# The root of a norm, by a logarithm and an exponential on ScalarE instead of a square root on ScalarE and a reciprocal on VectorE

## The chip, the core and the metric

The kernel runs on one core of a Trainium2 chip. Its metric is the device time of one execution in microseconds (us), the median of several. Five engines work side by side, each with its own queue that it takes strictly in order: TensorE (PE, and PEld for its weight loads), VectorE (DVE), ScalarE (ACT), GpSimd (POOL) and SyncE (SP), the last two mostly issuing transfers. ScalarE looks a function up in a table; a row named ACT_TABLE_LOAD is the instruction that puts another table in place.

## What is computed

Two layers of a hybrid attention and expert network over 512 latent tokens and 256 context tokens of width 1024. What the change touches is the norm, used for rows, for the low-rank projections and for every head:

```python
def rms_norm(x, g):
    x32 = x.astype(jnp.float32)
    y = x32 * lax.rsqrt(jnp.mean(x32 * x32, axis=-1, keepdims=True) + EPS)
    return (y * g.astype(jnp.float32)).astype(x.dtype)
```

Each layer: norm and modulation of the tokens, one input projection, latent attention (queries and keys normed per head) and windowed attention (likewise), softmaxes, an output projection, a second norm with modulation, and then expert retrieval: a product-key search picks 16 of 16384 experts for each of 8 heads, whose rows of `u` and `v` are gathered, dotted with the token and added up. For some token tiles all experts are computed densely instead.

## The kernel before

Tokens go in tiles of 128 (two of context, four latent). A layer has two parts.

The **first part** runs generators for each tile: `KV` and `Q` (norm, projection, low-rank step, head norms, transposes into `kT`, `qT`, `skT`, `sqT`), `A` (attention: scores, `soft`, transposes, values), `O` (output projection, second norm), `R` (product-key search, L606 to L653) and `G` (the choice of experts). Which instruction stands where in each engine's queue is decided by a scheduler when the program is built; the code's order is only its starting point. In the same part the gathered expert rows (L752 to L776) run whenever a tile has made its choice: POOL issues one indirect gather per row (L754), DVE makes the dot with the token (L758, `gv`) or the weighted sum (L768, `vacc`). Layer 0 starts with no such rows to do, since no tile has chosen; layer 1 begins with 40 rows left over from layer 0 and then has none until its first tile has chosen.

The **second part** of a layer streams all experts (L858 on) for the dense tiles, with the remaining gathered rows in between, in an order written out by hand. There are no norms in it.

All 88 norms end in one helper, `rstd_of` (L239): a square root on ACT with the mean and the epsilon folded into scale and bias (L241), then a reciprocal in place on DVE (L242). Before it, the sum of squares comes either from one ACT instruction with an accumulator (`rms_rows`, L249, tile `ss`, 44 norms: 22 of token rows in `modulated_T`, 22 in `low`) or from a Square on ACT and a sum on DVE (`heads_ss`, L328 and L330, tile `hss`, 44 norms of heads). After it, DVE either makes a diagonal matrix (`diag`, L255), with which PE scales and transposes in one go (L265, L346), or multiplies the heads (L405, L407, L422, L452, L455, L465). In `low`, ACT copies the projection out of PSUM (L338) right after the norm, and that copy frees the bank into which PE makes the next tile's projection (L372).

Other functions on ACT: Exp in the softmax (`soft`, L484 and L487) and in the choice (L727), Gelu (L761, L924), Silu once (L161), and Copy, Identity, Square, Abs and Relu, which never have a load of their own in this program.

Of the kernel before, what the change touches and what calls it, by code (L numbers as in the profile page):

```python
# [30 lines left out]
AF = mybir.ActivationFunctionType  # L31
# [58 lines left out]
def body(ctx: ExitStack, tc: tile.TileContext, I, out):  # L90
    nc = tc.nc
# [46 lines left out]
    eps_t = cst.tile([P, 1], F32, name="eps_t")  # L138
# [99 lines left out]

    def rstd_of(ss, n):  # L239

        nc.scalar.activation(ss, ss, AF.Sqrt, bias=eps_t, scale=1.0 / n)  # L241
        nc.vector.reciprocal(ss, ss)  # L242
        return ss

    def rms_rows(src, n, junk=None):
        if junk is None:
            junk = tm("upd", (P, D), BF)
        ss = sm.tile([P, 1], F32, tag="ss", name="ss")
        nc.scalar.activation(junk[:, :n], src, AF.Square, accum_out=ss)  # L249
        return rstd_of(ss, n)  # L250
# [129 lines left out]
    def project_kv(l, st, tiles, aT, K, kv):  # L380
# [9 lines left out]
        for j, i in enumerate(tiles):  # L390
            kt = kb + i
            krs, x, dg = xs[j]
            pb = low_rank(x, dg, KVR, K["kva_g"], w2, 512)
            nc.scalar.activation(kv["v"][:, kt, :], pb[:, 512:1024], AF.Copy)
            ss = heads_ss(pb[:, :512].rearrange("p (h w) -> p h w", w=NOPE), H, NOPE)
            s1 = sm.tile([P, 1], F32, tag="ss", name="ss")
            j2 = sm.tile([P, ROPE], F32, tag="j2", name="j2", bufs=2)
            nc.scalar.activation(j2, krs[:, 0, :], AF.Square, accum_out=s1)
            nc.vector.tensor_scalar(ss, ss, s1, None, op0=OP.add)
            rs = rstd_of(ss, QK)  # L400
            q = tm("q", (P, H, QK))
            kr = krs
            if st == "lat":
                kr = rope(krs, 1, "m", i, K["g_mk"])
            nc.vector.tensor_tensor(q[:, :, :NOPE], pb[:, :512].rearrange("p (h w) -> p h w", w=NOPE),  # L405
                                    rs.unsqueeze(2).to_broadcast([P, H, NOPE]), OP.mult)
            nc.vector.tensor_tensor(q[:, :, NOPE:], kr.to_broadcast([P, H, ROPE]),  # L407
                                    rs.unsqueeze(2).to_broadcast([P, H, ROPE]), OP.mult)
            heads_T(q, kv["kT"], slice(kt * P, (kt + 1) * P), K["mk_" + st])
            yield  # L410
        w, cn = in_w(l, "sk")
        for j, i in enumerate(tiles):
            kt = kb + i
            ps = proj(aT[j], w, cn)
            nc.scalar.activation(kv["sv"][:, kt, :], ps[:, 128:256], AF.Copy)
            k_ = tm("q", (P, 2, SD))
            nc.vector.tensor_copy(k_.rearrange("p h w -> p (h w)"), ps[:, :128])
            rs = rstd_of(heads_ss(k_, 2, SD), SD)
            src = rope(k_, 2, "s", i, K["g_sk"]) if st == "lat" else k_
            kd = tm("lowr", (P, 2, 2, SD), bufs=QB)  # L420
            for d_ in range(2):
                nc.vector.tensor_tensor(kd[:, :, d_, :], src, rs.unsqueeze(2).to_broadcast([P, 2, SD]), OP.mult)  # L422
            pt = m1()
            for g in range(2):
                nc.tensor.transpose(pt[:, g * P:(g + 1) * P], kd[:, g].rearrange("p d w -> p (d w)"), ident)
            nc.scalar.activation(kv["skT"][:, :, kt * P:(kt + 1) * P], pt[:, :2 * P].rearrange("p (g t) -> p g t", t=P),
                                 AF.Copy, scale=1.0 if st == "lat" else K["sk_ctx"])
            yield
# [565 lines left out]
    for l in range(L):  # L994
# [90 lines left out]
        with ExitStack() as es:  # L1085
# [3 lines left out]
            n = 256 * len(js)  # L1089
# [70 lines left out]
```

## Time and profile before

| | us |
|---|---|
| median of 3 runs | 4492.85 |
| lowest and highest of them | 4483.92 and 4502.79 |
| the profiled execution | 4481.78 |
| its span (first to last instruction) | 4480.0 |
| DVE busy in it | 3352.5 |
| ACT busy in it | 1687.4 |

A row of a page or of an answer names a line (L241 is line 241), an engine, the operation and the tiles, written tile first. The idle time of an engine before an instruction, and what ended it, stands behind an arrow. The chain of waits is followed back from the last instruction: at each step to what released it, or, if it waited for nothing, to the instruction ahead of it on its engine. A piece of the chain that names a DVE instruction can therefore mean that DVE was the bound there, or only that its queue had come to that point.

### The profile page before, as it was taken

To read this page: it belongs to the slowest core of one execution; us is meant where nothing else is said; L and a number is where in the kernel's file an instruction comes from. 1 tells how busy PE (TensorE), PEld (TensorE's weight loads), DVE (VectorE), ACT (ScalarE), POOL (GpSimd) and SP (SyncE) were. 2 spreads that over 40 slices of the span, in tenths; PEclk is the share of its full clock that TensorE was granted. 3 is DMA by queue.
4 is the path that set the end of the run, shared out by engine and by line. 5 is a ranking of instruction groups with operands and counts; after the bars stand their busy time and mean duration, and the time that the engine had idled before them with its cause. 6 is when DMAs were issued, how large, how long until landed. Compare 5 with 4: busy or idle time off the path is not lost.

```text
span 4480.0 us, 58044 instructions
## 1 busy us (share of the span) xinstructions
PE 3617.1 (81%) x19934; PEld 2907.9 (65%) x19934; DVE 3352.5 (75%) x7566; ACT 1687.4 (38%) x3244; POOL 1629.0 (36%) x1402
## 2 busy tenths in 40 slices
PE   6885778477887999999999668676676468999997
PEld 2453357256776898888988545444455467888886
DVE  1247778989678788777877832778989977777777
ACT  1342231155575333333333234232224653444443
POOL 2016565544101444444444510255443443222222
PEclk8997788788997999999999889898888579999999
DMA  8588898888666999999999952789899789889897
GB/s 303 171 284 305 307 346 310 299 300 311 219 204 229 327 318 315 325 334 328 332 311 318 330 175 92 258 320 336 310 335 345 260 307 337 301 298 304 298 316 245
DMA packets 467481, 1306.48 MB, mean 292 GB/s; under 512 B 41568, under 2 KB 147808, under 8 KB 467184
## 3 DMA queue, kind: packets, MB, share of 16 engines
q0 software_dynamic: 199744, 726.26, 46.0%
q1 hardware_dynamic: 267440, 576.50, 37.0%
q8 instruction: 157, 2.57, 0.2%
q14 instruction: 140, 1.15, 0.1%
HBM read 1240.70 MB, written 61.90 MB: 291 GB/s over the span
## 4 chain that ended last, share of the span: by engine, by line
PE 24%; issue 24%; DVE 23%; DMA 13%; ACT 8%; POOL 7%; SPq 0%; POOLq 0%; ACTq 0%; DVEq 0%
DVE vacc L768 8%; POOL gv L754 7%; PE m L644 5%; DVE v L868 4%; ACT u L867 3%; DMA gv<-v,idx 3%; DVE gv L758 2%; DMA gv<-u,idx 2%; PE m L372 2%; DMA raw<-uT 2%; PE acc L852 2%; PE A L921 2%; DMA w<-w_in 2%; PE o L894 2%; PE m L507 1%
## 5 line engine op out<-in xcount | busy, mean ns | idle before, releaser
L754 POOL DMA_INDIRECT gv<-v,idx x640 | 782.1, 1222 | 1143.4 <-DVE vacc L768 807.3
L754 POOL DMA_INDIRECT gv<-u,idx x640 | 784.6, 1226 | 964.3 <-DVE a L758 635.4
L894 PE MATMUL o<-v,W 128*128 128x512 f32 x3840 | 943.0, 398 | 71.3 <-ACT W L867 71.0
L921 PE MATMUL A<-b,u 128*128 128x384 f32 (+1 forms) x6144 | 962.5, 313 | 41.6 <-ACT w L924 29.8
L921 PEld LDWEIGHTS A<-b,u 128*128 128x128 f32 x6144 | 936.3, 192 | 70.8 <-ACT w L924 39.3
L894 PEld LDWEIGHTS o<-v,W 128*128 128x128 f32 x3840 | 719.0, 191 | 228.9 <-ACT W L867 84.6
L768 DVE SCALAR_TENSOR_TENSOR vacc<-gv,a,vacc 128x1024 f32<-128x1024 f32 x635 | 811.2, 1277 | 55.7 <-DMA gv<-v,idx 48.5
L758 DVE CUSTOM_DVE_ANT_0 gv<-gv,btok 128x1024 f32<-128x1024 f32 x640 | 768.0, 1218 | 98.0 <-DMA gv<-u,idx 97.1
L867 ACT ACTIVATE W<-w 128x384 fp32r<-128x384 f32 (+1 forms) x256 | 120.7, 472 | 1042.5 <-DVE w L927 1042.5
L868 DVE TENSOR_TENSOR u<-raw,u 128x1024 fp32r<-128x1024 f32 x256 | 313.5, 1224 | 166.3 <-ACT u L867 164.1
L372 PE MATMUL m<-w,aT 128*128 128x256 f32 (+3 forms) x704 | 259.7, 518 | 86.7 <-DMA w<-w_in 51.4
L644 PE MATMUL m<-bT,wq 128*128 128x128 f32 x2560 | 313.7, 279 | 5.0 <-DMA wq<-wq 4.1
L868 DVE TENSOR_TENSOR v<-raw,v 128x1024 fp32r<-128x1024 f32 x256 | 311.9, 1218 | 3.6 <-ACT v L867 3.5
L644 PEld LDWEIGHTS m<-bT,wq 128*128 128x128 f32 x2560 | 301.1, 195 | 10.7 <-DMA wq<-wq 5.7
L867 ACT ACTIVATE u<-raw 128x1024 fp32r<-128x1024 f32 x256 | 267.7, 1046 | 62.5 <-DMA raw<-uT 62.5
L867 ACT ACTIVATE v<-raw 128x1024 fp32r<-128x1024 f32 x256 | 267.4, 1044 | 4.6 <-PE o L894 4.5
L372 PEld LDWEIGHTS m<-w,aT 128*128 128x128 f32 x704 | 142.7, 213 | 190.5 <-DMA w<-w_in 69.2
L868 DVE TENSOR_TENSOR W<-w,W 128x384 fp32r<-128x384 f32 (+1 forms) x256 | 125.7, 491 | 144.7 <-ACT W L867 144.6
L927 DVE TENSOR_TENSOR w<-w,G 128x192 f32<-128x192 f32 (+1 forms) x512 | 143.6, 319 | 68.4 <-DMA G<-Gd 55.2
L852 PE MATMUL acc<-o,o 128*128 128x128 f32 x768 | 140.0, 337 | 66.8 <-ACT ar L853 60.0
L504 ACT ACTIVATE peT<-m 128x512 f32<-128x512 f32 (+1 forms) x192 | 109.5, 576 | 220.0 <-PE m L507 114.3
L536 PE MATMUL big<-kT,qT 96*128 96x256 f32 (+1 forms) x288 | 132.2, 593 | 71.9 <-ACT pexp L484 36.0
(215 smaller groups left out, 4286.0 us busy)
## 6 DMA issues: line engine op xcount, KB each, us to landing
raw<-uT SPq DMA_DIRECT2D x256, 512.0 KB, 5.6
raw<-v SPq DMA_DIRECT2D x256, 512.0 KB, 5.4
wq<-wq SPq DMA_DIRECT2D x144, 512.0 KB, 6.8
gv<-ada_w POOLq DMA_DIRECT2D x80, 512.0 KB, 6.7
Gd<-ar SPq DMA_DIRECT2D x80, 512.0 KB, 4.3
w<-w_out SPq DMA_DIRECT2D x72, 512.0 KB, 6.6
G<-Gd SPq DMA_DIRECT2D x16, 1536.0 KB, 12.4
G<-Gd SPq DMA_DIRECT2D x16, 1024.0 KB, 9.8
```

The costliest lines, as they stand in the source:

```text
L372: nc.tensor.matmul(ps[:, :cn], aT[:, k, :], w[k][:, :cn], start=(k == 0), stop=(k == KC - 1))
L536: nc.tensor.matmul(ps[:, k0:k0 + n], qT[:, h, :], kv["kT"][:, h, k0:k0 + n], start=True, stop=True)
L644: nc.tensor.matmul(ps[:, c], w[:, k, :], bT[:, k, :], start=(k == 0), stop=(k == KC - 1))
L754: return t, nc.gpsimd.indirect_dma_start(out=t, out_offset=None, in_=src, in_offset=bass.IndirectOffsetOnAxis(ap=idx[:, k:k + 1], axis=0))
L758: ins = nc.vector.tensor_tensor_reduce(out=t, in0=t, in1=bt, scale=1.0, scalar=0.0, op0=OP.mult, op1=OP.add, accum_out=a[:, k:k + 1])
L768: return nc.vector.scalar_tensor_tensor(acc, t, w[:, k:k + 1], acc, op0=OP.mult, op1=OP.add)
L852: nc.tensor.matmul(ps[:, x * NK:(x + 1) * NK], o1[:, x], o2, start=True, stop=True)
L867: nc.scalar.activation(hi, x, AF.Copy)
L868: nc.vector.tensor_tensor(lo, x, hi.bitcast(F32), OP.subtract)
L894: nc.tensor.matmul(acc[t][x], W[:, a_, c], v[:, b_, x * 512:(x + 1) * 512], start=(e == 0 and (a_, b_) == PARTS[0]), stop=(e == NK - 1 and ...
L921: nc.tensor.matmul(A, u[:, a_, k * P:(k + 1) * P], b[:, b_, k], start=(k == 0 and (a_, b_) == PARTS[0]), stop=(k == KC - 1 and (a_, b_) == ...
L927: nc.vector.tensor_tensor(wv[:, x], wv[:, x], gc[x][:, :, e % GC, :], OP.mult)
```

## The change

The helper takes the logarithm in the same place and with the same scale and bias, and then an exponential of minus half of it, also on ACT and also in place. The reciprocal on DVE is gone.

```diff
     def rstd_of(ss, n):
 
-        nc.scalar.activation(ss, ss, AF.Sqrt, bias=eps_t, scale=1.0 / n)
-        nc.vector.reciprocal(ss, ss)
+        nc.scalar.activation(ss, ss, AF.Ln, bias=eps_t, scale=1.0 / n)
+        nc.scalar.activation(ss, ss, AF.Exp, scale=-0.5)
         return ss
```

The ACT queue of the built program holds 52 table loads before: 23 ahead of L241, 19 ahead of L484, 4 of L727, 1 of L487, and 5 of Gelu and Silu. After, it holds 182: 88 ahead of L241, 87 ahead of L242, 2 ahead of L484, and the same 5.

The first place is on ACT, in the first key projection of layer 0, where `low` norms two context tiles (`lowr` is the copied projection, `krs` the rotary key, `j_342` scratch):

```order
 L249 ACTIVATE lowr,ss<-m_283 128x256
+L241 ACT_TABLE_LOAD
 L241 ACTIVATE ss<-ss,eps_t 128x1
 L338 ACTIVATE lowr<-m_283 128x256
+L242 ACT_TABLE_LOAD
+L242 ACTIVATE ss<-ss 128x1
 L249 ACTIVATE lowr,ss<-m_302 128x256
 L398 ACTIVATE j_342,ss<-krs 128x32
 L349 ACTIVATE lowT<-m_325,gcols 128x128 x2
+L241 ACT_TABLE_LOAD
 L241 ACTIVATE ss<-ss,eps_t 128x1
```

A load now stands ahead of the logarithm and another ahead of the exponential; the copy L338 stands between the two.

The second place is on ACT too, where the last head norm of the context queries lies between two pairs of softmax exponentials (`pexp` are the exponentials, `su` their sums):

```order
-L484 ACT_TABLE_LOAD
 L484 ACTIVATE pexp,su<-big,nb 128x256 x2
 L241 ACT_TABLE_LOAD
 L241 ACTIVATE hss<-hss,eps_t 128x8
-L484 ACT_TABLE_LOAD
+L242 ACT_TABLE_LOAD
+L242 ACTIVATE hss<-hss 128x8
 L484 ACTIVATE pexp,su<-big,nb 128x256 x2
```

Here the load ahead of the second pair has moved up to the norm's own exponential, and the load ahead of the first pair is gone.

The third place is on DVE, at the first of these two: the reciprocals between the sums and their users.

```order
 L387 COPY krs<-m_283 128x32
-L242 RECIPROCAL ss<-ss 128x1
 L255 TENSOR_SCALAR diag<-ident,ss 128x128
 L387 COPY krs<-m_302 128x32
-L242 RECIPROCAL ss<-ss 128x1
 L255 TENSOR_SCALAR diag<-ident,ss 128x128
 L330 TENSOR_REDUCE hss<-pexp 128x8
 L399 TENSOR_SCALAR hss<-hss,ss 128x8
-L242 RECIPROCAL hss<-hss 128x8
 L405 TENSOR_TENSOR q<-big,hss 128x8x64
```

DVE's queue keeps its order and loses only the reciprocal; what stood behind it, the diagonal or the product, now waits for ACT itself.

## Rows read from the trace of the kernel before

**Rows 1.** The page, its first part: busy us, share of the span, instructions.

```profile
PE 3617.1 (81%) x19934; PEld 2907.9 (65%) x19934; DVE 3352.5 (75%) x7566; ACT 1687.4 (38%) x3244; POOL 1629.0 (36%) x1402
```

**Rows 2.** Windows, reciprocals of L242 alone: stretch, length, busy (count), clock, DMA.

```profile
0.00:320.00 320.00, 3.01 (x17) 0.93 0.72 253
320.00:1400.00 1080.00, 5.31 (x31) 0.82 0.80 282
2540.00:2840.00 300.00, 4.83 (x28) 0.87 0.52 180
```

**Rows 3.** Chain of waits (start, us, what): ACT pieces, first and last each.

```profile
122.20 0.03 ACT ss L241
...
2711.16 0.31 ACT hss L241
...
166.28 1.28 ACT L484
...
2905.47 1.28 ACT L484
```

**Rows 4.** Chain of waits: the first and last piece with a reciprocal.

```profile
106.25 0.17 DVE hss L242
...
3066.96 0.11 DVE hss L242
```

**Rows 5.** Groups by line on ACT, table loads (count, busy us, mean ns, idle).

```profile
L241 ACT ACT_TABLE_LOAD x23 | 29.5, 1283 | 0.4
L484 ACT ACT_TABLE_LOAD x19 | 24.4, 1283 | 2.0 <-DVE nb L480 1.7
L727 ACT ACT_TABLE_LOAD x4 | 5.1, 1283 | 0.1
```

**Rows 6.** Timeline of ACT at the norm between two softmaxes (start, us).

```profile
168.40 0.20 ACT L484 ACTIVATION_READ_ACCUMULATOR pexp<-big,nb 128x1 f32 x1
168.61 1.28 ACT L241 ACT_TABLE_LOAD   x1
169.91 0.30 ACT L241 ACTIVATE hss<-hss,eps_t 128x8 f32<-128x8 f32 x1
170.22 1.28 ACT L484 ACT_TABLE_LOAD   x1
```

**Rows 7.** Chain of waits through a head norm without a load.

```profile
136.93 0.31 ACT hss L241
...
137.26 0.21 DVE hss L242
...
137.50 0.97 DVE q L455
```

**Rows 8.** Groups by line: an ACT instruction without pointer operands, and the reciprocals.

```profile
L398 ACT ACTIVATE j<-krs 128x32 f32<-128x32 f32 x12 | 2.7, 227 | 2.4 <-DVE diag L255 2.4
...
L242 DVE RECIPROCAL hss<-hss 128x8 f32<-128x8 f32 (+1 forms) x44 | 8.2, 187 | 11.9 <-ACT hss L241 11.9
L242 DVE RECIPROCAL ss<-ss 128x1 f32<-128x1 f32 x44 | 7.0, 160 | 82.6 <-ACT ss L241 82.6
```

**Rows 9.** Chain of waits through a norm in `low`.

```profile
2698.62 0.29 ACT ss L241
...
2698.91 0.28 ACT lowr L338
...
2701.47 5.52 DMA w<-wukv
```

**Rows 10.** Timelines of ACT and DVE: two square roots and their reciprocals.

```profile
413.91 0.30 ACT L241 ACTIVATE hss<-hss,eps_t 128x8 f32<-128x8 f32 x1 [2.04 <-DVE hss L399]
...
414.93 0.20 DVE L242 RECIPROCAL hss<-hss 128x8 f32<-128x8 f32 x1
...
3017.82 0.29 ACT L241 ACTIVATE ss<-ss,eps_t 128x1 f32<-128x1 f32 x1
...
3027.26 0.16 DVE L242 RECIPROCAL ss<-ss 128x1 f32<-128x1 f32 x1
```

## The prediction

> **What bounds the kernel now.** I read the page first. No engine is full: PE 81% of the span, DVE 75%, ACT 38% [rows 1]. ACT has room on average, so a dearer norm costs only where something waits for it. Then I counted the norms by stretch, with windows that show the reciprocals alone: 17 in the first 320 us, where no gathered rows run, 31 from 320 to 1400 us beside gathered rows, 28 from 2540 to 2840 us at the head of layer 1, almost without gathered rows [rows 2]; the other 12 of the 88 follow up to 3400 us. The second parts of both layers have none and are left alone. Last I went through the chain of waits over all these stretches. ACT's L241 stands on it 22 times: 11 times with a table load ahead of the instruction, 11 times without, the first and the last of these at 122.20 and 2711.16 us [rows 3]. A further 19 norms without a load are on it by their reciprocal alone, the first at 106.25 and the last at 3066.96 us [rows 4]. So of the 65 norms that have no load of their own today (88 less the 23 loads of L241 [rows 5]) 30 touch the chain and 35 don't.
>
> **What is removed.** 88 reciprocals on DVE, 8.2 + 7.0 = 15.2 us busy [rows 8]; and of the softmax's and the choice's loads (19 and 4 [rows 5], and one of L487) 22, since the exponential of a norm leaves their table in place.
>
> **What is added.** The built program says it, not the diff: a load ahead of each logarithm (88 instead of 23) and a load ahead of 87 of the 88 exponentials. The two functions do not share a table here. That is 65 + 87 - 22 = 130 loads more, or two for each of the 65 norms that had none. A load takes 1283 ns [rows 5]. It starts 0.01 us after the instruction ahead of it ends and the next begins 0.02 us after it, 1.30 us from start to start [rows 6]. In that row and in its like it begins after what its own instruction waits for, so it is not hidden in a wait. 130 x 1.30 = 169 us more on ACT, whose 1687 us leave room for it; the question is the path.
>
> [...]
>
> **The price of one norm without a load today.** Before: the root starts at 136.93, the reciprocal 0.33 us later, the product that uses it at 137.50: 0.57 us [rows 7]. After: load 1.30, logarithm 0.31 (the same form as the root, 169.91 to 170.22 [rows 6]), load 1.30, exponential. The trace has no exponential of 1 to 8 elements without pointer operands; the nearest row is a Square of 32 elements, 227 ns [rows 8], and I take 0.23, and 0.03 for the hand-over to DVE as with the root. 3.17 in all, 2.6 us more. In `low` the way to PE leaves by the copy L338 (2698.62, 2698.91 [rows 9]), which stands behind the logarithm's load but ahead of the exponential's: there the price is 1.3.
>
> **The sum, by classes.**
> - *On the chain through ACT, 11 norms.* 6 leave by L338 (1.3 each), 5 by DVE (2.6 each): 7.8 + 13.0 = 20.8 us.
> - *On the chain by the reciprocal alone, 19 norms.* Here the root was done some time before DVE came to it, and that slack is taken off 2.6. Four have at most 0.04 us: 10.4. Three have more than 2.6, as 3017.82 + 0.29 to 3027.26 [rows 10]: nothing. Twelve lie between, as 413.91 + 0.30 to 414.93, slack 0.72, price 1.9 [rows 10]; taken one by one they give 14.7. Together 25.1.
> - *The 11 chain norms that have a load already.* They gain the exponential's load, 1.3 each, except the one that leaves by L338: 13. Against it go eight loads of L484 that lie on the chain (166.28 the first, 2905.47 the last [rows 3]): 8 x 1.28 = 10.3, if all are among the 17 that vanish. Net 2.7.
> - *The other 35.* Their slack is not in the chain view. Lower end nothing, upper end 35 x 2.6 = 91. The 30 of the first two classes cost 46 of at most 78, some six tenths, because they are on the path already. These are not, and I take a sixth, 15 us. The nearest row is the waiting of DVE before reciprocals, 82.6 + 11.9 us [rows 8]: DVE does stand waiting for these results in many places, so not zero.
> - *The reciprocals gone from DVE* are inside the 2.6 where they are on the path; elsewhere they are worth at most the 15.2 us of their busy time, and I count nothing, since DVE now waits at that point for the exponential.
>
> 20.8 + 25.1 + 2.7 + 15 = 64 us. On the profiled execution, 4481.78, that is 4546. That execution lies 11 us under the median of the runs shown, so against the median, 4492.85, I forecast **4557 us**, 1.4% more.
>
> What hides the rest: PE making the second tile's projection while the first tile's norm goes on, and the gathered rows in DVE's queue. If this cover is gone, each uncovered norm costs up to its 2.6. What is late next where a stall grows is the transfer of weights. After the norm at 2698.62 the chain waits 5.52 us for `wukv` [rows 9], whose buffers come free only as PE proceeds, so that wait moves along more than it absorbs; but where the weights were late for their own reasons, it absorbs. That could take half of the first three classes, and is the lower end.
>
> **The rivals.**
> - *Everything is hidden.* Gathered rows and weights absorb all but a third: 4493 + 21 or less, so within 0.5% (22 us, about what a measurement of this kernel can tell from no change). For it: the slack of the three norms above and the 5.52 us. Against it: half of the norms lie in stretches without gathered rows, 17 + 28 of 88 [rows 2].
> - *Every switch is on the path.* Tile pairs push each other back on ACT, so all 65 pay: 169 + 3 = 172, 4665 us. For it: the products follow in all cases. Against it: 35 norms are not on the chain.
> [...]
> - *The change does what it says, and the result is faster.* If logarithm, exponential and softmax were served from one table, the loads left would be those of Gelu and Silu and the returns from Gelu, some 9 of 52. On the chain 11 loads of L241 and 8 of L484 would go, 19 x 1.30 = 25 us: 4493 - 25 = 4468. It decides as soon as no load stands between logarithm and exponential. [...] No row before shows a logarithm; the built program, with 87 loads ahead of L242, speaks against it.
>
> **How the numbers follow.** Forecast 0.73, hidden 0.12, all on the path 0.08, draining 0.03, one table 0.04. Slower by over 0.5%: 0.73 + 0.08 + 0.03 = 0.84; within 0.5%: 0.12; faster by over 0.5%: 0.04. The range goes from half of the first three classes and nothing of the fourth (4493 + 24, rounded to 4515) to all of the fourth (4557 + 76 = 4633, rounded to 4630); it takes in the draining and leaves out the two outer cases and a part of the hidden one.
>
> **What would show it.** Right: loads at L241 and L242 of 88 and 87 with 1283 ns each, two or so at L484; ACT busy up by some 170 to 190 us (130 loads and 88 exponentials of 0.2); the head of layer 1 and the first 320 us longest in the change, about 25 to 30 and 10 to 15 us; the stretches with experts alone unchanged in length; the chain with pieces of L242 on ACT. Wrong: few loads at L242 (one table); a gap ahead of each load (draining); stretches without gathered rows that grow by less than 10 us together (hidden) or by more than 60 (all on the path); or a second part that changes in length, which no step here foresees.

## The result, and the profile after

| us | before | after |
|---|---|---|
| median of 4 runs | 4489.33 | 4541.88 |
| lowest and highest | 4483.92, 4502.79 | 4539.45, 4552.15 |
| the profiled execution | 4481.78 | 4539.45 |
| its span | 4480.0 | 4537.7 |

The ratio is 1.0125, 95% interval 1.0109 to 1.0140: the kernel became slower by 49 to 63 us, 53 by the medians. The forecast was 4557 us and slower; the time lies 15 us under it and inside the range.

The page of the kernel after, the row that answers to [rows 1]:

```profile
PE 3640.6 (80%) x19934; PEld 2919.0 (64%) x19934; DVE 3344.2 (74%) x7478; ACT 1874.2 (41%) x3462; POOL 1668.3 (37%) x1402
```

ACT is busy 1874.2 us instead of 1687.4, 186.8 more. It still stands free for more than half of the span. The groups of the kernel after on ACT say where the 186.8 come from (count, busy us, mean ns, then idle time before them and what ended it):

```profile
L241 ACT ACT_TABLE_LOAD x88 | 112.9, 1283 | 1.5
L242 ACT ACT_TABLE_LOAD x87 | 111.6, 1283 | 1.5
L242 ACT ACTIVATE hss<-hss 128x8 f32<-128x8 f32 (+1 forms) x44 | 9.2, 208 | 0.5
L242 ACT ACTIVATE ss<-ss 128x1 f32<-128x1 f32 x44 | 8.9, 203 | 0.5
L484 ACT ACT_TABLE_LOAD x2 | 2.6, 1283 | 0.0
```

With the 5 loads of Gelu and Silu that is 182, against 52 in [rows 5]: 130 more at 1283 ns are 166.8 us, and the 88 exponentials are 18.1. The exponential of 1 to 8 elements takes 203 to 208 ns. The idle time before all 175 loads is 3.0 us together: they follow what stands ahead of them at once.

The stretches come from the first and last start of a line. Kernel before: the reciprocal L730 of the first choice of experts, the first dense matmul L921 of layer 0, the first search L644 of layer 1 (least, median and most ns, then first and last start):

```profile
L730 DVE RECIPROCAL gs<-gs x6: 183/188/195, 326.3 to 1395.5; 128x8 f32<-128x8 f32 x6
L921 PEld LDWEIGHTS A<-b,u x3072: 186/188/333, 1401.2 to 2503.9; 128*128 128x128 f32 x192
L644 PEld LDWEIGHTS m<-bT,wq x1024: 186/192/333, 2810.4 to 3446.4; 128*128 128x128 f32 x171
```

Kernel after, the same lines:

```profile
L730 DVE RECIPROCAL gs<-gs x6: 200/228/272, 344.9 to 1426.2; 128x8 f32<-128x8 f32 x6
L921 PEld LDWEIGHTS A<-b,u x3072: 186/188/333, 1431.2 to 2534.0; 128*128 128x128 f32 x192
L644 PEld LDWEIGHTS m<-bT,wq x1024: 186/192/333, 2874.6 to 3505.5; 128*128 128x128 f32 x171
```

The first choice comes 18.6 us later, the dense part of layer 0 30.0, the first search of layer 1 64.2. Both kernels were profiled a second time among the experiments, so something of the scatter is known too. The stretches in us; left out are the 30 to 36 us between the dense part of layer 0 and the head of layer 1, and 11 to 12 at the end. The head of layer 1 goes from its first norm (L249) to its first search:

| | before | before again | after | after again |
|---|---|---|---|---|
| start to first choice | 326.3 | 330.3 | 344.9 | 339.8 |
| to the dense part of layer 0, beside gathered rows | 1074.9 | 1079.7 | 1086.3 | 1086.8 |
| dense part of layer 0 | 1114.9 | 1116.7 | 1115.7 | 1118.1 |
| head of layer 1 | 264.1 | 265.9 | 295.0 | 297.0 |
| to the dense part of layer 1, beside gathered rows | 829.2 | 838.9 | 825.2 | 831.1 |
| dense part of layer 1 | 829.2 | 823.0 | 825.9 | 828.8 |

By the means of each pair the first stretch lost 14 us, the stretch after it 9, the head of layer 1 31. The last but one is 6 us shorter, which is less than the 10 us between two profiles of the same kernel. The dense parts didn't move.

One more thing differs between the two kernels, and it bears on the experiments. What was said of DVE's queue ahead of the prediction, that it keeps its order, holds at the place shown there and not for the whole program. Here is DVE at the end of the first stretch, before:

```profile
264.43 0.28 DVE L255 TENSOR_SCALAR diag<-ident,ss 128x128 f32<-128x128 f32 x1
265.88 0.16 DVE L488 TENSOR_TENSOR su<-su,es 128x1 f32<-128x1 f32 x1 [1.17 <-ACT es L487]
```

And after, where the diagonal has gone behind the sums:

```profile
282.60 0.16 DVE L488 TENSOR_TENSOR su<-su,es 128x1 f32<-128x1 f32 x1 [1.37 <-ACT es L487]
...
283.58 0.28 DVE L255 TENSOR_SCALAR diag<-ident,ss 128x128 f32<-128x128 f32 x1
```

Laid side by side in the traces, without the loads and the norm's own two instructions, the queues of ACT and DVE are the same up to this place and, but for three instructions, in the head of layer 1. Beside gathered rows they are not: some 440 of DVE's instructions stand elsewhere in layer 0 and some 340 in layer 1, and some 150 and 90 of ACT's. So a difference between two kernels is a price of loads alone only where their orders agree.

What the head of layer 1 looks like inside is shown by the chain of waits of the kernel after through one context tile (start, us, what):

```profile
2673.90 0.52 ACT lowT L349 x2
2674.42 0.02 issue
2674.43 1.28 ACT L241
2675.72 0.01 issue
2675.73 0.30 ACT ss L241
2676.02 0.27 ACT lowr L338
2676.29 0.02 issue
2676.31 1.28 ACT L242
2677.59 0.01 issue
2677.61 0.21 ACT ss L242
2677.82 0.02 issue
2677.84 0.30 DVE diag L255
2678.14 0.02 issue
2678.16 0.33 ACT j L398 x2
2678.49 0.48 ACT v L394
2678.97 0.49 ACT pexp L328
2679.46 0.02 issue
2679.47 1.28 ACT L241
2680.76 0.01 issue
2680.77 0.30 ACT hss L241
2681.07 0.02 issue
2681.09 1.28 ACT L242
```

Two norms, four loads, all on the chain: in 9 us ACT itself has become the path, and 5.1 us of it are loads. Lines without a tile (`ACT L241`) are the loads. In the whole stretch from 2580 to 2875 us, L241 and L242 hold 7.0 and 6.1% of the chain, 39 us.

### The profile page after: what moved, and what is told of

Read it like the earlier page. It is cut to its first block, busy times and chain, and to the rows that moved or that the text cites. A ratio compares the mean times of both kernels' runs of the same rounds, so it can differ in the third digit from the quotient of the medians.

```text
span 4537.7 us, 58199 instructions
## 1 busy us (share of the span) xinstructions
PE 3640.6 (80%) x19934; PEld 2919.0 (64%) x19934; DVE 3344.2 (74%) x7478; ACT 1874.2 (41%) x3462; POOL 1668.3 (37%) x1402
## 4 chain that ended last, share of the span: by engine, by line
PE 33%; DVE 25%; issue 14%; DMA 12%; ACT 12%; POOL 3%; SPq 1%; ACTq 0%; DVEq 0%; POOLq 0%
DVE vacc L768 9%; PE A L921 6%; PE o L894 6%; PE m L644 4%; DVE v L868 4%; ACT u L867 4%; POOL gv L754 3%; DVE gv L758 3%; DMA raw<-uT 3%; DMA gv<-u,idx 3%; DMA gv<-v,idx 3%; PE m L372 2%; PE acc L852 2%; ACT ar L853 2%; DVE w L927 2%
## 5 line engine op out<-in xcount | busy, mean ns | idle before, releaser
L754 POOL DMA_INDIRECT gv<-v,idx x640 | 802.7, 1254 | 1162.0 <-DVE vacc L768 826.5
L754 POOL DMA_INDIRECT gv<-u,idx x640 | 802.4, 1254 | 939.0 <-DVE a L758 598.5
L894 PE MATMUL o<-v,W 128*128 128x512 f32 x3840 | 946.8, 399 | 78.9 <-ACT W L867 77.9
L921 PE MATMUL A<-b,u 128*128 128x384 f32 (+1 forms) x6144 | 956.1, 311 | 33.4 <-ACT w L924 24.5
L921 PEld LDWEIGHTS A<-b,u 128*128 128x128 f32 x6144 | 930.3, 191 | 62.1 <-ACT w L924 33.0
L768 DVE SCALAR_TENSOR_TENSOR vacc<-gv,a,vacc 128x1024 f32<-128x1024 f32 x635 | 814.7, 1283 | 51.3 <-DMA gv<-v,idx 43.3
L644 PE MATMUL m<-bT,wq 128*128 128x128 f32 x2560 | 312.9, 279 | 2.0 <-DMA wq<-wq 1.4
L644 PEld LDWEIGHTS m<-bT,wq 128*128 128x128 f32 x2560 | 301.0, 195 | 7.2 <-issue 3.1
L480 DVE TENSOR_REDUCE nb<-big 128x1 f32<-128x768 f32 (+3 forms) x160 | 122.6, 769 | 103.8 <-PE big L536 52.0
```

The source lines that it names most:

```text
L480: nc.vector.tensor_reduce(nb, ps[:, :n], AX.X, OP.max, negate=True)
L644: nc.tensor.matmul(ps[:, c], w[:, k, :], bT[:, k, :], start=(k == 0), stop=(k == KC - 1))
L754: return t, nc.gpsimd.indirect_dma_start(out=t, out_offset=None, in_=src, in_offset=bass.IndirectOffsetOnAxis(ap=idx[:, k:k + 1], axis=0))
L768: return nc.vector.scalar_tensor_tensor(acc, t, w[:, k:k + 1], acc, op0=OP.mult, op1=OP.add)
L894: nc.tensor.matmul(acc[t][x], W[:, a_, c], v[:, b_, x * 512:(x + 1) * 512], start=(e == 0 and (a_, b_) == PARTS[0]), stop=(e == NK - 1 and ...
L921: nc.tensor.matmul(A, u[:, a_, k * P:(k + 1) * P], b[:, b_, k], start=(k == 0 and (a_, b_) == PARTS[0]), stop=(k == KC - 1 and (a_, b_) == ...
```

## The experiments

### One table for all of it

At the end of the file the logarithm and the exponential are taken out of every set of tables that the compiler is offered but one. The program then has 9 loads instead of 182. Nothing else differs from the kernel after; the traces show ACT and DVE in the same order throughout.

```diff
+_tables = _hw.get_activation_tables
+
+def _one_table(*args, **kwargs):
...
+            v.discard(AF.Ln)
+            v.discard(AF.Exp)
...
+_hw.get_activation_tables = _one_table
```

> The changed kernel with one thing altered in how it is built: only the table that holds both functions is offered for the logarithm and the exponential, so the program holds 9 table loads instead of 182 (before: 52). The instructions are the same. Theory (the loads are the whole cost): the 58 us go, and so do the 11 loads of L241 and 8 of L484 that lay on the chain of the kernel before, 19 x 1.30 = 25 us: some 25 us faster than before, ratio 0.993 to 0.997. Rival (the second function on ScalarE, and DVE waiting for it in order, is what costs): still slower than before by 10 us or more, ratio above 1.002.

Measured: 4450.87 us, ratio to the kernel before 0.9934 (0.9907 to 0.9961). By the ratios that is 30 us less than before and some 86 less than after. Groups of this kernel on ACT, all its loads:

```profile
L241 ACT ACT_TABLE_LOAD x3 | 3.8, 1283 | 0.1
L761 ACT ACT_TABLE_LOAD x2 | 2.6, 1283 | 0.0
L924 ACT ACT_TABLE_LOAD x2 | 2.6, 1283 | 12.1 <-PE A L921 12.1
L161 ACT ACT_TABLE_LOAD x1 | 1.3, 1283 | 0.8 <-PEq L1153 0.8
L484 ACT ACT_TABLE_LOAD x1 | 1.3, 1283 | 0.0
```

Nine loads, and the same two instructions per norm, in the same order, as in the kernel after. So the loss of the change is the loads, not the longer way over ACT; and the idea of the change holds as soon as the loads are really gone. One set can serve both functions, as the 9 loads show, but here it did so only when it alone was on offer; in the kernel after there are 182. This version is faster than both kernels.

### Taking the loads away, keeping the reciprocal

```diff
     def rstd_of(ss, n):
 
-        nc.scalar.activation(ss, ss, AF.Sqrt, bias=eps_t, scale=1.0 / n)
+        nc.scalar.activation(ss, ss, AF.Identity, bias=eps_t, scale=1.0 / n)
         nc.vector.reciprocal(ss, ss)
```

> The kernel before with the root's function replaced by Identity, with the same operands (the norms come out wrong), and the reciprocal left on DVE: 9 table loads, as in the run with one table, and no second function on ScalarE. Theory (loads alone decide, the move from DVE to ScalarE is worth nothing): within 7 us of the run with one table, which was 30 us faster than before: ratio 0.992 to 0.995. Rival (the reciprocals taken from DVE are worth their 15 us where DVE is full): 10 to 15 us slower than the run with one table, ratio 0.996 to 0.997.

Measured: 0.9961 (0.9945 to 0.9977), 17 us under before. That lies in the rival's range, and its interval reaches into the theory's. The order of ACT and DVE is that of the kernel before, so the 17 us (10 to 25) are what its 43 loads cost. The 12 us that part it from the one-table kernel can't be put down to the reciprocal that left DVE: the one-table kernel has the other order of the queues as well, and the two intervals overlap from 0.9945 to 0.9961. What either is worth isn't separated from nothing.

With these two kernels the change comes apart: 17 us less without the 43 loads, 12 less for the move to ACT and the other order together, 86 more for the 173 loads by which the kernel after differs from the one-table kernel. That is 57 us, as the ratio 1.0125 has it.

### A third load

A Gelu stands between logarithm and exponential, with a load of its own: for the 28 norms at the head of layer 1 the trace has 28 loads each at L241, L242 and L243.

```diff
         nc.scalar.activation(ss, ss, AF.Ln, bias=eps_t, scale=1.0 / n)
+        nc.scalar.activation(ss, ss, AF.Gelu)
         nc.scalar.activation(ss, ss, AF.Exp, scale=-0.5)
```

> The changed kernel with a Gelu put in place between the logarithm and the exponential of every norm (its output is wrong, the norms are not norms any more): a third load, 88 more, with an instruction of 0.2 us, so 1.5 us more for each norm. Theory (a load costs only where the cover of the norm is used up): the first 130 loads cost 58 us, 0.43 us each; the next come on norms whose cover is partly gone, so more each, 0.6 to 0.9: 53 to 80 us above the changed kernel, 110 to 135 above before. Rival 1 (all the switches are on the path): 134 us above the changed kernel. Rival 2 (what costs is only a changed order of the queues): within 15 us of the changed kernel.

Measured: 1.0301 (1.0269 to 1.0333), 135 us over before and 79 over after. The 88 instructions and loads are 88 x 1.5 = 134 us of ACT's time (1283 ns, and 203 to 206 for the function at the head of layer 1), and six tenths of it show in the end. The rival by which all of it lies on the path falls, and so does the one by which the order alone did it. The next load costs a larger share than the first two did (53 of 185 us), as it would if they had used up a part of the cover. The order of the queues differs here too, though hardly in the head of layer 1 (six instructions of DVE).

How it goes in the head of layer 1 is read from windows over that stretch: from and to, length, busy us of PE, PEld, DVE, ACT and POOL with counts, mean granted clock, DMA share, GB/s. The one-table kernel:

```profile
2527.00:2785.00 258.00, 188.58 (x895) 125.15 (x896) 94.07 (x211) 104.50 (x294) 27.38 (x24) 0.89 0.48 165
```

The kernel before:

```profile
2546.00:2810.00 264.00, 195.83 (x895) 129.91 (x896) 97.60 (x239) 105.12 (x270) 29.00 (x25) 0.87 0.48 163
```

The kernel after:

```profile
2580.00:2875.00 295.00, 205.15 (x901) 135.30 (x902) 93.23 (x211) 176.67 (x350) 29.19 (x24) 0.83 0.43 144
```

The kernel with a third load:

```profile
2617.00:2949.00 332.00, 213.19 (x900) 141.23 (x901) 93.57 (x211) 218.62 (x406) 27.35 (x24) 0.78 0.38 129
```

ACT's busy time grows by 71.6 us from before to after and the stretch by 31; by 42 more with the third load, and the stretch by 37. The first step is paid at four tenths, the second at nine.

### The change in a part of the norms

Six kernels make the change in some norms only; a flag in the helper chooses, and it is switched where the next generators are started. The edit of the first of them, against the kernel after:

```diff
+    fresh = [True]
+
     def rstd_of(ss, n):
 
-        nc.scalar.activation(ss, ss, AF.Ln, bias=eps_t, scale=1.0 / n)
-        nc.scalar.activation(ss, ss, AF.Exp, scale=-0.5)
+        if fresh[0] == True:
+            nc.scalar.activation(ss, ss, AF.Ln, bias=eps_t, scale=1.0 / n)
+            nc.scalar.activation(ss, ss, AF.Exp, scale=-0.5)
+        else:
+            nc.scalar.activation(ss, ss, AF.Sqrt, bias=eps_t, scale=1.0 / n)
+            nc.vector.reciprocal(ss, ss)
         return ss
...
                 run(KVQ(c, 0, 1))
+                fresh[0] = False
...
+                fresh[0] = True
                 run(KV(c, 0, 1), KV(t, 0, 1), Q(t, 0), left, KV(t, 2, 3), A(t, 0), O((t, 0)))
+                fresh[0] = False
                 run(RF(t, 0), Q(t, 1), A(t, 1))
```

That one has the 42 norms that run with hardly any gathered rows beside them (14 in the first context pass of layer 0, 28 at the head of layer 1):

> The change in 42 of the 88 norms only, those of the first context pass of layer 0 and of the first projections of layer 1, where hardly any gathered rows run beside them; the other 46 keep root and reciprocal. 126 table loads, 74 more than before. Theory (cover by gathered rows and by the second tile decides): the first choice and the first search of layer 1 came 18.6 and 31 us later by the two traces, so 45 to 52 us of the 58, ratio 1.010 to 1.012. Rival (each load costs alike): 58 x 74 / 130 = 33 us, ratio 1.007.

With the flag turned round, the other 46:

> The complement: the change in the 46 norms that have gathered rows beside them, root and reciprocal in the 42 others. 108 table loads, 56 more than before. Theory (cover decides): 3 to 12 us, ratio 1.0005 to 1.003. Rival (each load costs alike): 58 x 56 / 130 = 25 us, ratio 1.0055.

Measured: 1.0075 (1.0052 to 1.0099) for the 42 and 1.0030 (1.0014 to 1.0047) for the 46. Equal prices for all norms put the 46 at 1.0055, or 1.0051 by the 53 us of the medians, just outside. But the 42 cost less than the cover theory wanted (1.010 to 1.012); they came out where the rival had them. The two together, 1.0105, are less than the whole, though not clear of the intervals. The trace of the 42 shows where: the first choice came at 338.5 us, 8 to 12 later than before, the dense part of layer 0 at 1401.7, not later at all. The stretch between was 12 us shorter, little more than it scatters. The next four kernels take that apart.

The 14 norms of the first pass alone (the second and third switch are left out):

> The change is made only in the 14 norms of the first context pass of layer 0 (22 table loads more than before); the other 74 norms keep root and reciprocal. Theory (the gathered-row stretch behind it makes up for what this pass loses, as long as it has no loads of its own): the first choice comes 10 to 14 us later than before, the dense part of layer 0 starts within 5 us of before, and the time is 0 to 6 us above before, ratio 1.000 to 1.0013. Rival (what is lost there stays lost): dense part of layer 0 10 to 14 us later, ratio 1.0022 to 1.0031.

The 34 norms of layer 0 after it (the flag turned round, the third switch left out):

> The change is made only in the 34 norms of layer 0 after its first context pass (44 table loads more than before); first pass and layer 1 keep root and reciprocal. The first pass alone measured 0.9978 and all of layer 0 1.0045. Theory (both draw on one slack: a first pass that ends later is made up only while this stretch has no loads of its own): ratio 1.000 to 1.003, so that the two parts alone sum to less than the whole by 0.003 or more. Rival (each part has its own price): 1.0055 to 1.008, the whole less the first pass alone.

All 48 of layer 0 (the helper asks for the layer instead of the flag):

> The change is made in all 48 norms of layer 0 and none of layer 1 (68 table loads more than before). Theory (the first pass and the gathered-row stretch draw on the same slack, so together they cost more than each alone): dense part of layer 0 starts 20 to 28 us later than before, ratio 1.0045 to 1.0062, more than the first pass alone and the covered norms alone give in sum. Rival (each norm has its price, whatever the others do): ratio within 0.001 of the sum of the excess of the first pass alone and 0.001 to 0.0015 for the 34 covered norms of layer 0.

The 28 at the head of layer 1 (the flag off at the start):

> The change is made only in the 28 norms at the head of layer 1, from its first norm to its first search (52 table loads more than before). Theory (this stretch has no cover, and nothing behind it makes up for it): head of layer 1 292 to 298 us long instead of 264 to 266, time 28 to 34 us above before, ratio 1.006 to 1.0076. Rival (the stretch behind it makes up for a part, as in layer 0): head as long, but ratio under 1.0055.

| the change in | norms | loads more | ratio | first choice | dense part of layer 0 |
|---|---|---|---|---|---|
| none (two profiles) | 0 | 0 | 1 | 326.3, 330.3 | 1401.2, 1410.0 |
| first pass of layer 0 | 14 | 24 | 0.9978 (0.9964 to 0.9991) | 336.8 | 1409.0 |
| rest of layer 0 | 34 | 44 | 1.0012 (0.9997 to 1.0028) | 328.4 | 1408.6 |
| all of layer 0 | 48 | 68 | 1.0045 (1.0026 to 1.0063) | 339.9 | 1420.8 |
| head of layer 1 | 28 | 50 | 1.0061 (1.0046 to 1.0076) | 325.4 | 1397.3 |
| rest of layer 0, and the last 12 | 46 | 56 | 1.0030 (1.0014 to 1.0047) | 328.2 | 1410.1 |
| all (two profiles) | 88 | 130 | 1.0125 and 1.0129 | 344.9, 339.8 | 1431.2, 1426.6 |

The loads are counted in the traces; for the first pass and the head of layer 1 the expectations have 22 and 52.

In layer 0 neither part costs anything by itself, 0.9978 and 1.0012, and both together cost 0.0045, 20 us, where the sum of the parts is -0.0010. That is what the theory foresaw, a slack on which both parts draw. It isn't shown, because the order of the queues is a rival. The kernel with the first pass alone has the order of the kernel before only up to some 780 us; behind that, some 120 of DVE's instructions stand elsewhere in layer 0 and some 230 beside the gathered rows of layer 1, though no norm was changed there. What it lost in the first pass may have been made up by this order as well as by a slack, and its 0.9978, under all that was expected, may come from there too. Its profiled run, 4490.38 us, is the slowest of its 12, and shows no gain to look into.

One pair has the same order throughout, the rest of layer 0 and all of layer 0. They differ in the first pass alone: 1.0045 against 1.0012, 15 us (4 to 26). The first choice comes 12 us later, 339.9 against 328.4, and the dense part 12 us later too, 1420.8 against 1408.6. With the order held and the rest changed too, nothing of what the first pass lost was made up. Both readings allow that: the slack may be used up by the loads of the rest, or there may be none. No run has the changed first pass beside the order of the kernel before, so why it cost nothing alone stays open.

The head of layer 1 pays in full view: 298.1 us in that kernel against 264.1 and 265.9, with all but three instructions of ACT and DVE in the same order, and 27 us in the time. The rival, that the stretch behind makes up for a part, had under 1.0055, and the interval doesn't quite shut it out: by the point values some 6 us were made up. All of layer 0 and the head of layer 1 sum to 1.0106. What is left to 1.0125 are the other 12 norms of layer 1; the difference between the 46 and the 34 norms, 1.0030 - 1.0012, is 0.0018, and then the sum is 1.0124. With intervals of 0.0015 to 0.002 to either side of each term, so close an agreement is partly luck. One comparison stays loose: the 42 measured 1.0075, first pass and head of layer 1 alone sum to 1.0039; the intervals overlap, but only at the rim.

### The copy ahead of the norm

In `low`, the copy L338 is put ahead of the logarithm's load, so that the bank comes free before any load.

```diff
-        dg = diag(rms_rows(ps[:, :n], n, x))
-        nc.scalar.activation(x[:, :n], ps[:, :n], AF.Copy)
-        return x, dg
+        ss = sm.tile([P, 1], F32, tag="ss", name="ss")
+        nc.scalar.activation(x[:, :n], ps[:, :n], AF.Square, accum_out=ss)
+        nc.scalar.activation(x[:, :n], ps[:, :n], AF.Copy)
+        return x, diag(rstd_of(ss, n))
```

> The changed kernel with the copy out of PSUM in the low-rank step put ahead of the logarithm's load instead of behind the logarithm; 180 or so loads as in the changed kernel. Theory (the price at the norms of the low-rank step is the one load that stands ahead of that copy): six such norms lay on the chain of the kernel before, so 6 x 1.3 = 8 us less than the changed kernel, against 0.3 us a norm for the later logarithm: 4 to 8 us faster than it. Rival (that copy is not what PE waits for): within 3 us of the changed kernel, or slower.

It ran beside the kernel after, taken once more:

> The changed kernel, once more, for a second profile and a closer interval. Ratio 1.011 to 1.014; the first 320 us 18 us longer and the head of layer 1 31 us longer than in the kernel before, both within 3 us if they are not scatter.

Measured: 1.0116 (1.0096 to 1.0135) beside 1.0129 (1.0109 to 1.0149). In the second profile of the kernel after the head is 31 to 33 us longer than before, as expected; the first stretch is 10 to 14 longer instead of 18, so a part of the 18.6 was scatter.

The 6 us between the two kernels are what the theory asked for, but the intervals cover each other, and beside gathered rows the queues stand in another order, so the time decides nothing. The trace doesn't show the gain where it should be: the head of layer 1, with the order unchanged, takes 296.2 us, against 295.0 and 297.0. The timeline of ACT there says why (lines behind the edit are one higher; L339 is the copy):

```profile
2604.44 0.37 ACT L339 ACTIVATE lowr<-m 128x256 f32<-128x256 f32 x1
2604.83 1.28 ACT L241 ACT_TABLE_LOAD   x1
2606.12 0.29 ACT L241 ACTIVATE ss<-ss,eps_t 128x1 f32<-128x1 f32 x1
2606.43 1.28 ACT L242 ACT_TABLE_LOAD   x1
2607.73 0.20 ACT L242 ACTIVATE ss<-ss 128x1 f32<-128x1 f32 x1
2608.28 0.23 ACT L399 ACTIVATE j<-krs 128x32 f32<-128x32 f32 x1 [0.35 <-DVE diag L255]
```

The copy is early, but the next norm's work on ACT stands behind both loads as before, and waits for the diagonal that needs the exponential.

### The kernel before, once more, without an edit

> The kernel before, once more, for a second profile: how far the length of each stretch moves from one execution to the next with nothing changed. If the stretches with gathered rows move by 10 us between executions, the 12 us by which the partial change shortened a stretch that it did not touch is scatter; if they repeat within 3 us, it is the order of the queues. Ratio 1.000.

Measured: 0.9996 (0.9979 to 1.0013); its stretches are in the table above. A stretch beside gathered rows scatters by 5 to 10 us between these two profiles, so the 12 us of the partial change are hardly more than scatter, and the order of the queues differs there besides. The head of layer 1 moves by 2 us here; over all six kernels and repeats whose head was not changed and that hold the loads of before there, it takes 259.5 to 267.7 us.

## Why the prediction was right, and where its sum was off

**Right.** The counts, the duration of a load, no gap ahead of it, 186.8 us more on ACT (170 to 190 foreseen), the exponential (203 to 208 ns for 0.23 us), the dense parts unchanged, the first stretch (14 us for 10 to 15). The mechanism is shown by the one-table kernel: with 9 loads instead of 182 the same instructions in the same order take 0.9934 of the time of before.

**No draining.** The chances give 0.03 to a draining of the engine at each load, and the range takes it in; no run shows such a term. What the kernel after shows in its place: the load at 2674.43 starts 0.02 us after the end of the instruction ahead of it (0.01 in [rows 6]), idle time before 175 loads is 3.0 us, and the logarithm starts 0.01 us after this load ends.

**Hidden, and all on the path.** Both are out: 53 us of 169 to 185. The truth lies between them, with somewhat more hidden than the sum had it: 64 us forecast, 53 measured by the medians (49 to 63), 58 between the two profiled executions. The forecast of 4557 was 15 us above 4541.88; 11 of them are this, and 3.5 come from the median of before, which moved from 4492.85 to 4489.33 with the fourth run.

**A load can hide in a wait.** The prediction said that a load begins after what its own instruction waits for. For the norms of heads this is wrong. The kernel before, the roots of heads, and what they waited for:

```profile
L241 ACT ACTIVATE hss<-hss,eps_t 128x8 f32<-128x8 f32 (+1 forms) x44 | 13.2, 299 | 78.9 <-DVE hss L330 45.1 <-DVE hss L399 33.7
```

The kernel after:

```profile
L241 ACT ACTIVATE hss<-hss,eps_t 128x8 f32<-128x8 f32 (+1 forms) x44 | 13.2, 301 | 33.0 <-DVE hss L399 16.6 <-DVE hss L330 16.0
```

ACT waited 78.9 us for DVE's sums of squares and now waits 33.0. The load runs in that time; where the sum is later still, the instruction waits behind its load, as here in the kernel after:

```profile
2612.42 1.28 ACT L241 ACT_TABLE_LOAD   x1
2615.72 0.30 ACT L241 ACTIVATE hss<-hss,eps_t 128x8 f32<-128x8 f32 x1 [2.02 <-DVE hss L399]
```

The sign of it stood in the prediction's own rows: 413.91 in [rows 10] has 2.04 us of waiting before the root, room for a whole load, and yet it was charged 1.9 of 2.6 us. The row on which the step was built [rows 6] is a place where ACT had not waited. So the price of a head norm is 2.6 less up to 1.3 of such a wait, and the three first classes were too dear there; by how much in all isn't measured.

**The stretches.** The first stretch and the head of layer 1 lost 14 and 31 us, 45 together where 35 to 45 stood. That leaves 19 to 29 of the 64 us for the stretches beside gathered rows, and these lost 9 and gained 6: 3 us, with a scatter of 5 to 10 each. So it is there that the sum was too high. Over the whole program DVE's waiting in the kernel after shows the other end of the norm, the diagonals:

```profile
L255 DVE TENSOR_SCALAR diag<-ident,ss 128x128 f32<-128x128 f32 x44 | 13.1, 298 | 158.0 <-ACT ss L242 158.0
```

The same group in the kernel before:

```profile
L255 DVE TENSOR_SCALAR diag<-ident,ss 128x128 f32<-128x128 f32 x44 | 12.7, 288 | 0.9
```

It is 158.0 us, for 82.6 before the reciprocals of rows [rows 8] and these 0.9: 74.5 us for 44 norms, 1.7 each. This is the full wait of DVE, not what the end pays.

**The classes and the order.** The 15 us of the fourth class, for the 35 norms off the chain, can't be checked by themselves. Where the classes lie is read from the chain of before: of the 19 norms on it by their reciprocal alone, 14 stand beside gathered rows, of the 35 off it 23 do not. So the term that was too large is, as far as the stretches tell, the second class, 25.1 us, most of which stood where 3 us were lost; the fourth may well be too small. That the total came within 11 us is in part luck. The prediction also reckoned with the order of the queues as it was, which holds in the head of layer 1 and not beside gathered rows. There the difference of the two kernels mixes the price of loads with that of another order, and no run separates them for the change as a whole.

**The copy L338.** The lower price of 1.3 us for the norms in `low` rests on the bank being what the path waits for. The experiment gave no clear gain from freeing it earlier, and the chain above goes on through the exponential's load and the diagonal. That step isn't confirmed.

**One table.** The rival's price was 25 us; the kernel with one table measured 30 (18 to 42). The built program had said that it would not be so here, and that was the right ground to give it 0.04.

## What to carry to other kernels

Before a function is exchanged for one "in the same table", count the loads in the built program: here the same kernel source gave 182 or 9, and the time went from 1.2% worse to 0.7% better. ACT was busy for 41% of the span with all the loads, and they were still paid where ACT was waited for, 31 us in the head of layer 1; where ACT itself was going to wait for its operand they ran in the wait, 78.9 us of it before the roots of heads and 33.0 after. So look at the idle time before the instruction as well as at the slack behind it. When a change is tried in parts, compare the order of the queues too: with the whole change the scheduler placed some 440 of DVE's instructions elsewhere in layer 0, and of the parts of layer 0 only the pair with the same order (1.0012 and 1.0045) told what one costs beside the other.

## What the hardware showed that was not expected

In the head of layer 1 the same matmuls cost PE 188.6, 195.8, 205.2 and 213.2 us in the four windows above (895 to 901 recorded matmuls), with a mean granted clock of 0.89, 0.87, 0.83 and 0.78: in these four the same work took the longer, the lower the mean. PE is busy 73, 74, 70 and 64% of these stretches: with more loads it stands idle longer in between, but the first two do not fit that order. Nor are the loads all of it. Two kernels with no change in that stretch, the 46 norms and the rest of layer 0, took 259.5 and 267.7 us there. PE's own busy time is 9 us longer after than before, at 0.83 instead of 0.87; how much of the 31 us that makes, and how much of it the stretch hides, no run separates.
